# Which engine waits for the last stores: the closing wait of a ReLU row-sum kernel put on VectorE in place of SyncE

## Chip, cores and metric

One core of one Trainium2 chip. The metric is the device time of an execution in microseconds. Every run whose state is on record was in the fast state, with a granted clock of 1.00; of the first six runs of the kernel before, only the profiled one lists more than its time. Each of the other runs also lists its span, the time from the first to the last recorded instruction, to 0.1 us. The time is always longer than the span; "time outside the span" below is the one minus the other, so in a single timed run it is only good to 0.05 us.

## The reference

```python
# x: 32 x 512 x 1024 float32
relu_x = np.maximum(x, 0)
return np.sum(relu_x, axis=-1)      # 32 x 512
```

## The kernel before

67 MB come in, 64 KB go out. SyncE issues all loads and stores; ScalarE clamps, VectorE sums, and near the end each takes single rows with a fused clamp and sum. The end of the program is written by hand, without the usual closing barrier. The parts that the change and the argument touch:

```python
    def store(m, n, act, dve):
        nonlocal n_store
        dst, src = sums(m, n)
        nc.sync.wait_ge(sems.act, act)
        nc.sync.dma_start(out=dst, in_=src).wait_op(sems.dve, dve, "sem-ge").then_inc(
            sems.stored, 16
        )
        n_store += 1
    # ... cut: loads, clamps, sums ...
    store(0, ROWS, *freed[0])
    store(ROWS, NT - ROWS - 2, *sums_done)
    # ... cut: VectorE's last pieces of the last row but one ...
    store(NT - 2, 2, n_act, n_dve)
    return n_store

# the end of the program (line 45 and line 46):
    nc.sync.sem_clear(cleared)                    # loads, act and dve back to 0
    nc.sync.wait_ge(sems.stored, 16 * n_stores).then_inc(sems.stored, -16 * n_stores)
```

Three stores raise `stored` by 16 each. The last line waits for 48 and takes the 48 off again, so that the next execution finds the semaphore at 0.

Of the kernel before, what the change touches and what calls it, by code (L numbers as in the profile page):

```python
# [25 lines left out]
def kernel(tc: tile.TileContext, x: bass.AP, out: bass.AP):  # L26
    nc = tc.nc
    sems = Semaphores(tc)

    tc.close()  # L30
    tc.compile()
    nc.cur_bb = nc.bb_map[tc.start_bb_name]
    body = nc.cur_bb.bb.instructions
    ends = list(body)
    body.clear()
    n_stores = relu_sum(nc, sems, x, out)
    body.extend(ends)


    nc.cur_bb = nc.bb_map[tc.start_bb_name + "_end"]  # L40
    nc.cur_bb.bb.instructions.clear()
    nums = sorted(s.num for s in (*sems.loads, sems.act, sems.dve))
    cleared = range(nums[0], nums[-1] + 1)
    assert len(cleared) == len(nums)
    nc.sync.sem_clear(cleared)
    nc.sync.wait_ge(sems.stored, 16 * n_stores).then_inc(sems.stored, -16 * n_stores)
    issue_ahead_of_the_barrier(tc, EARLY)


# [183 lines left out]
def issue_ahead_of_the_barrier(tc: tile.TileContext, n_loads: int):  # L233


    SP = mybir.EngineType.SP
    blocks = tc.nc.main_func.blocks
    opening = blocks[0].instructions
    body = next(b for b in blocks if b.name == tc.start_bb_name).instructions
    loads = [i for i in body if i.engine == SP][:n_loads]  # L240
    for i in loads:
        assert isinstance(i, mybir.InstDMACopy)
        body.remove(i)
    at = next(n for n, i in enumerate(opening) if i.engine == SP)
    opening[at:at] = loads
# [30 lines left out]
```

## Time and profile before

| | before |
|---|---|
| time, median (lowest to highest), 3 runs | 161.35 us (161.24 to 161.53) |
| span of the profiled run | 159.63 us |
| time of that same run | 160.99 us, so 1.36 us outside the span |
| last input has landed | about 155.3 us |
| last sum ready, last store issued | 158.17, 158.19 us |
| wait of line 46 begins, ends | 159.615, 159.632 us |

How to read it: the input stream fills the span up to 155 us, and some work on the last rows follows. From 158.2 us on no engine computes; the core waits for one 1 KB store to be confirmed. The bar of a wait shows only its last few nanoseconds, after the semaphore has been satisfied; the waiting itself has no bar and must be read from the gap before it. Outside the span no instruction is recorded and no view of the profile shows anything.

### The profile page before, as it was taken

How to read it: one execution, taken by the hardware profiler on the slowest of the kernel's cores; microseconds unless marked ns; L12 is line 12 of the kernel's file. 1: busy time of each engine (PE TensorE's matmuls, PEld its weight loads, DVE VectorE, ACT ScalarE, POOL GpSimd, SP SyncE). 2: the span in 40 equal slices, each digit the busy share in tenths (PEclk: the TensorE clock that was granted, in tenths of full speed). 3: DMA queues.
4: the chain of work that ended last, by engine and by line, in shares of the span. 5: the costliest groups of instructions: out<-in, count | busy, mean ns of one | idle time of the engine just before them, and what ended most of it. 6: DMA issues, size and time to landing. Idle time of an engine off the chain costs nothing.

```text
span 159.6 us, 129 instructions
## 1 busy us (share of the span) xinstructions
DVE 117.5 (74%) x41; ACT 104.2 (65%) x50; POOL 0.2 (0%) x4
## 2 busy tenths in 40 slices
DVE  0000000009999499994999999999999999999986
ACT  3000059990799708996099941999339992499985
POOL 0000000000000000000000000000000000000000
DMA  7996996996996998979969969969969969798994
GB/s 263 525 525 263 525 526 263 525 525 263 526 493 296 525 411 378 525 328 460 526 279 509 525 263 526 525 263 525 525 263 525 509 279 525 337 452 386 412 405 127
DMA packets 2304, 67.18 MB, mean 421 GB/s; under 512 B 640, under 2 KB 896, under 8 KB 1024
## 3 DMA queue, kind: packets, MB, share of 16 engines
q1 hardware_dynamic: 2304, 67.18, 98.1%
HBM read 67.11 MB, written 0.07 MB: 421 GB/s over the span
## 4 chain that ended last, share of the span: by engine, by line
DMA 43%; DVE 34%; ACT 17%; another core or an unknown queue 3%; SPq 0%; issue 0%; DVEq 0%
DMA io<-in_x_dram 43%; DVE res L123 32%; ACT io L115 17%; DVE io L140 1%; SPq L97 0%; DVE piece L219 0%; DVE piece L140 0%; DVEq L218 0%
## 5 line engine op out<-in xcount | busy, mean ns | idle before, releaser
L123 DVE TENSOR_REDUCE res<-io 128x8 f32<-128x8192 f32 (+2 forms) x9 | 101.1, 11286 | 39.9 <-ACT io L115 39.9
L115 ACT ACTIVATE io<-io 128x8192 f32<-128x8192 f32 (+2 forms) x9 | 81.7, 9111 | 46.9 <-DMA io<-in_x_dram 46.9
L130 ACT ACTIVATE io<-io 128x1024 f32<-128x1024 f32 x20 | 20.9, 1045 | 5.9 <-DMA io<-in_x_dram 5.7
L140 DVE TENSOR_SCALAR_CACHE_REDUCE io<-io 128x1024 f32<-128x1024 f32 (+1 forms) x14 | 15.5, 1165 | 0.7 <-DMA io<-in_x_dram 0.6
L130 ACT ACTIVATION_READ_ACCUMULATOR io<-io 128x1 f32 x20 | 3.8, 188 | 0.0
L115 ACT ACT_TABLE_LOAD x1 | 1.3, 1283 | 0.8 <-PEq L260 0.8
L140 DVE DVE_READ_ACCUMULATOR io<-io 128x1 f32 x14 | 1.2, 82 | 0.0
L219 DVE TENSOR_SCALAR_CACHE_REDUCE piece<-piece 128x406 f32<-128x406 f32 x1 | 0.6, 576 | 0.1
L140 DVE TENSOR_SCALAR_CACHE_REDUCE piece<-piece 128x260 f32<-128x260 f32 x1 | 0.4, 424 | 0.0
L260 POOL MEMSET const-bfloat16-1.0<- 128x1 bf16 x1 | 0.1, 102 | 0.0
L260 POOL MEMSET const-uint8-127<- 128x1 uint8 x1 | 0.1, 102 | 0.0
L260 POOL MEMSET const-float32-0.0<- 128x1 f32 x1 | 0.1, 99 | 0.2 <-issue 0.2
L260 POOL MEMSET const-float32-1.0<- 128x1 f32 x1 | 0.1, 99 | 0.0
L140 DVE DVE_READ_ACCUMULATOR piece<-piece 128x1 f32 x1 | 0.1, 83 | 0.0
L219 DVE DVE_READ_ACCUMULATOR piece<-piece 128x1 f32 x1 | 0.1, 82 | 0.0
## 6 DMA issues: line engine op xcount, KB each, us to landing
io<-in_x_dram SPq DMA_DIRECT2D x1, 4096.0 KB, 21.6
io<-in_x_dram SPq DMA_DIRECT2D x1, 2048.0 KB, 26.1
io<-in_x_dram SPq DMA_DIRECT2D x1, 1204.0 KB, 28.6
io<-in_x_dram SPq DMA_DIRECT2D x1, 512.0 KB, 29.4
piece<-in_x_dram SPq DMA_DIRECT2D x1, 202.0 KB, 29.3
piece<-in_x_dram SPq DMA_DIRECT2D x1, 130.0 KB, 29.3
io<-in_x_dram SPq DMA_DIRECT2D x7, 26.9
out_dram<-res SPq DMA_DIRECT2D x1, 55.0 KB, 1.6
```

Of the source, the lines that this page charges most:

```text
L115: i = nc.scalar.activation(out=ap, in_=ap, func=RELU)
L123: nc.vector.tensor_reduce(out=res[:, m : m + n], in_=ap, axis=mybir.AxisListType.X, op=ADD).wait_op(sems.act, n_act, "sem-ge").then_inc(se ...
L130: i = nc.scalar.activation(out=ap, in_=ap, func=RELU, accum_out=res[:, m : m + 1])
L140: i = nc.vector.tensor_scalar(out=ap, in0=ap, scalar1=0.0, scalar2=None, op0=MAX, op1=ADD, accum_out=accum_out,)
L219: nc.vector.tensor_scalar(out=last[:, :], in0=last[:, :], scalar1=0.0, scalar2=None, op0=MAX, op1=ADD, accum_out=res[:, NT - 2 : NT - 1],) ...
L260: nc = _bacc.Bacc("TRN2", target_bir_lowering=False, num_devices=1)
```

## The change

The closing wait moves from SyncE's queue to VectorE's. VectorE has nothing left to do by then, and SyncE, which issued the stores, is freed about a microsecond sooner.

```diff
     nc.sync.sem_clear(cleared)
-    nc.sync.wait_ge(sems.stored, 16 * n_stores).then_inc(sems.stored, -16 * n_stores)
+    nc.vector.wait_ge(sems.stored, 16 * n_stores).then_inc(sems.stored, -16 * n_stores)
     issue_ahead_of_the_barrier(tc, EARLY)
```

## The prediction

> **What bounds the kernel now.** I read the head of the page first, then the chain that ended last, then the last stretch of the timeline, then the waits of SyncE's queue, then the single line that the change edits.
>
> ```profile
> span 159.6 us, 129 instructions
> DMA 43%; DVE 34%; ACT 17%; another core or an unknown queue 3%; SPq 0%; issue 0%; DVEq 0%
> DMA io<-in_x_dram 43%; DVE res L123 32%; ACT io L115 17%; DVE io L140 1%; SPq L97 0%; DVE piece L219 0%; DVE piece L140 0%; DVEq L218 0%
> ```
>
> These are the span and the chain, by engine and by line. The chain is the loads of x, ScalarE's clamp (L115) and VectorE's row sums (L123): 43 + 32 + 17 = 92% of the span. Over the span the DMA moves 67.18 MB at a mean of 421 GB/s, and its row of 40 slices stands at 9 almost everywhere, so the input stream sets the length up to about 155.4 us. The change touches none of that. It edits one instruction behind the last store, so only the last few microseconds are of interest. The timeline of them:
>
> ```profile
> 157.37 0.08 DVE L140 DVE_READ_ACCUMULATOR piece<-piece 128x1 f32 x1
> 157.58 0.58 DVE L219 TENSOR_SCALAR_CACHE_REDUCE piece<-piece 128x406 f32<-128x406 f32 x1
> 158.09 0.08 DVE L219 DVE_READ_ACCUMULATOR piece<-piece 128x1 f32 x1
> 158.19 0.33 SPq L108 DMA_DIRECT2D out_dram<-res  x1
> ```
>
> VectorE's last result is there at 158.09 + 0.08 = 158.17. SyncE issues the last store, of 1 KB, at 158.19. VectorE has nothing more to do, and ScalarE has finished before it. The waits of SyncE's queue in this stretch:
>
> ```profile
> SPq L107 <- ACT io L130: 28.2, 2, 27.3
> SPq L46 <- SPq L46: 1.0, 1, 1.0
> SPq L108 <- DVE piece L219: 0.3, 1, 0.3
> ```
>
> L46 is the line that changes. It waits 1.0 us, once. The view names the queue itself as the releaser, which cannot be literally true: what raises the semaphore is the landing of the last store, as the program says (three stores of 16 each, and the wait is for 48). The instruction itself:
>
> ```profile
> L46 SPq EVENT_SEMAPHORE  x1: 17/17/17, 159.6 to 159.6; - x1
> ```
>
> It takes 17 ns and begins when the wait is over: the trace puts its start at 159.615 and its end at 159.632, which is the end of the span. So the last 1.46 us of the span (158.17 to 159.63) are: 0.03 us to release the issue, about 1.42 us from the issue of the last store to the semaphore (the list of DMA issues has 1.4 for this store), 17 ns for the wait. SyncE's other instruction in that time, the range clear of L45, begins at 158.57 and takes 57 ns; it is over 0.99 us before the semaphore is full. It is hidden.
>
> **What the skill says.** The Trainium skill, page "DMA: Bandwidth & Descriptors", section "Anatomy of one DMA — SWDGE (gpsimd) path", puts most of a DMA's fixed cost of about 2 us into the receipt of the write at the target, which must come before the semaphore is raised. The trace agrees in kind: in this 1 KB store the packets run from about 0.83 us to 1.03 us after the issue began, and the semaphore is full 0.39 us later; the sum is 1.42 us and not 2.0. None of it depends on who waits.
>
> The page "Perfetto Trace Analysis", section "Sequencer-only Instruction (DRAIN, etc)", says that the profile shows such an instruction from the moment its semaphores are satisfied, so neither the wait nor the spreading of its own update is in the bar. The trace agrees: L46 is a bar of 17 ns behind a wait of 1.0 us. A wait on VectorE would be of the same kind.
>
> The page "Runtime: NRT & Kernel Launch", section "The ~15µs preamble/postamble breakdown", says that behind the kernel comes a barrier in which all engines meet (about 1.5 us), then a reset of semaphores, and that the serpentine over the five engines costs 44 ns a hop, some 355 ns in all. The trace shows no instruction behind L46, so it can neither confirm nor deny this. What it does show: the profiled run was timed at 160.99 us with a span of 159.63, so 1.36 us of the time lie outside the span, and what stands there is unknown to me.
>
> **The change, part by part.**
>
> Removed: one SyncE wait, 17 ns at the end of the span. Added: one VectorE wait with the same semaphore, threshold and decrement. VectorE's sequencer has done such a wait already:
>
> ```profile
> L218 DVEq EVENT_SEMAPHORE  x1: 21/21/21, 157.5 to 157.5; - x1
> ```
>
> 21 ns, against 17 on SyncE: +4 ns. The other cost is how fast each engine sees the semaphore. The opening barrier releases them in one go: SyncE's wait begins at 0.708, ScalarE's at 0.713, VectorE's at 0.719 from the start of the span, so VectorE is 11 ns later. A second comparison: the wait of L218 begins 38 ns after VectorE's read of 157.37 ended, and SyncE's store 28 ns after VectorE's last: 10 ns again. So the added end is 4 + 11 = +15 ns inside the span: 159.63 to about 159.65. VectorE is free from 158.17, its sequencer has only a branch left, and the semaphore comes at 159.6: it will be waiting in good time, with 1.4 us to spare. No reduction is delayed, because the wait stands behind the last one in VectorE's order.
>
> Moved: SyncE is now finished at about 158.57 + 0.06 = 158.63 and not at 159.63, 1.0 us sooner; VectorE is finished at 159.65 and not at 158.17. The last engine to finish does so at the same moment within 15 ns. The order on memory is unchanged: the range clear still comes behind the last store's own waits, and the stores' semaphore is still taken down only after all have landed. I see no race.
>
> Sum inside the span: +0.015 us, that is +0.01%. Outside the span: unknown in sign. If the engines meet afterwards in a chain, it matters how far along the chain the last engine stands, and whether SyncE has something of its own to do before it. By the skill's figure for the whole serpentine I estimate at most 0.35 us either way. A change like this in a tuned kernel is tried because someone hopes for exactly that, so I lean slightly to a gain, -0.06 us, a judgement and not a working. 161.35 + 0.015 - 0.06 is about 161.3 us.
>
> **Rivals.**
>
> First, SyncE's freedom is worth the whole 1.0 us: it would do work of its own behind the kernel while the store still flies. For it: 1.36 us outside the span are unexplained, and SyncE carries all DMA queues of this kernel. Against it: whatever ends the program must wait for VectorE too, and the store's landing is as late as before. It would give about 160.3 us, still within 1%. I give it under one in twenty.
>
> Second, VectorE is a worse place: the meeting point passes it early and must now go round again, or the first instructions behind the kernel are slower to come on VectorE than on SyncE. For it: SyncE was quickest to answer in the opening barrier, and the order of the others followed by 5, 6 and 2 ns. Against it: all those differences are tens of nanoseconds. It would give up to 161.35 + 0.35 = 161.7 us.
>
> Third, nothing changes outside the span, and the time is 161.35 + 0.015, 161.37 us, which three runs cannot tell from before. This is the likeliest of the three.
>
> None of them puts a load or a reduction on another schedule, because the edit lies behind all of them. That is also why no new bound can appear: VectorE is at 74% of the span and gets 21 ns more.
>
> **Range and chances.** The three runs before lie between 161.24 and 161.53, and the profiled run at 160.99; the spread of the same program is therefore 0.54 us, more than the effect that I expect. A median of three runs should move by less, some 0.2 us, and the unknown part outside the span adds up to 0.35 either way. I put the range at 160.85 to 161.7 us. The threshold of 2% is 3.2 us, more than twice the whole stretch from the last store's issue to the end; no way of this change leads there. Faster by over 2%: 0.005; within 2%: 0.99; slower by over 2%: 0.005.
>
> **What would show it.** In the profile after: a wait of about 21 ns on VectorE's queue as the last record, 1.4 us after the issue of the last store, and SyncE's last record the range clear; the span 159.6 to 159.7 unless the loads themselves ran differently; everything before 158 the same. The step outside the span is judged by the difference between the timed run and its span, 1.36 us now: if it is lower by several tenths, the first rival holds; if higher, the second. The prediction is wrong if the time leaves the range; then the cause must lie outside the span, or in a wait on VectorE that begins much later than 30 ns after the landing.

## The result and the profile after

| | before | after |
|---|---|---|
| time, median (lowest to highest) | 161.34 us (161.16 to 161.53), 6 runs | 161.38 us (161.30 to 161.59), 6 runs |
| ratio | | 1.0004, 95% interval 0.9992 to 1.0017 |
| span of the profiled run | 159.63 us | 159.81 us |
| time outside the span, that run | 1.36 us | 161.30 - 159.81 = 1.49 us |
| last store issued to wait begins | 1.420 us | 1.433 us |

A ratio here and below is the mean time of one kernel's runs over the mean of the other's of the same rounds, so it is not quite the ratio of the medians that stand beside it.

The head and the chain of the page of the kernel after, in shares of the span:

```profile
span 159.8 us, 129 instructions
DMA 43%; DVE 34%; ACT 17%; another core or an unknown queue 3%; SPq 0%; issue 0%; DVEq 0%
```

The same count of instructions and the same chain. The last microseconds of its timeline (start, length, engine, line, operation):

```profile
157.75 0.58 DVE L219 TENSOR_SCALAR_CACHE_REDUCE piece<-piece 128x406 f32<-128x406 f32 x1
158.25 0.08 DVE L219 DVE_READ_ACCUMULATOR piece<-piece 128x1 f32 x1
158.36 0.33 SPq L108 DMA_DIRECT2D out_dram<-res  x1
```

All three bars stand 0.16 us later than before (157.75 against 157.58) and are as long as they were. That shift has nothing to do with the edit. It is already there at the first load, whose semaphore is full at 21.71 us before and at 21.86 after. The chain in order of time, first of the kernel before and then of the kernel after:

```profile
0.79 40.24 DMA io<-in_x_dram
```

```profile
0.79 40.40 DMA io<-in_x_dram
```

The first load in the chain, which starts 159 us ahead of the edited instruction, took 40.40 us in place of 40.24. One profile against one profile thus shows a difference of 0.18 us in the span, of which 0.16 are the chance of the input stream. With an effect this small, measure from the last common event, here the issue of the last store, and not from the start.

The edited line of the kernel after:

```profile
L46 DVEq EVENT_SEMAPHORE  x1: 21/21/21, 159.8 to 159.8; - x1
```

It is on VectorE's queue and takes 21 ns, where it took 17 on SyncE. The trace puts its start at 159.792, its end at 159.813, the end of the span. The waits of SyncE's queue in the last five microseconds, after:

```profile
SPq L107 <- ACT io L130: 28.2, 2, 27.3
SPq L108 <- DVE piece L219: 0.3, 1, 0.3
```

The line "SPq L46 <- SPq L46: 1.0" that the prediction showed is gone. No line for it appears among VectorE's waits, though VectorE's queue stands idle from about 158.3 to 159.8. The landing did not become quicker; this view merely does not count the wait there.

What remained to explain was the other number, 1.49 us outside the span against 1.36, from one profiled run of each.

### The profile page after: what moved, and what is told of

It is laid out like the page before. It is cut to its first block, busy times and chain, and to the rows that moved or that the text cites. A ratio compares the mean times of both kernels' runs of the same rounds, so it can differ in the third digit from the quotient of the medians.

```text
span 159.8 us, 129 instructions
## 1 busy us (share of the span) xinstructions
DVE 117.5 (74%) x41; ACT 104.2 (65%) x50; POOL 0.2 (0%) x4
## 4 chain that ended last, share of the span: by engine, by line
DMA 43%; DVE 34%; ACT 17%; another core or an unknown queue 3%; SPq 0%; issue 0%; DVEq 0%
DMA io<-in_x_dram 43%; DVE res L123 32%; ACT io L115 17%; DVE io L140 1%; SPq L97 0%; DVE piece L219 0%; DVE piece L140 0%; DVEq L218 0%
```

## The experiments

All were run with repeated rounds beside the kernel before, on the same chip within a group. The groups ran on three chips. The kernel before had, outside its span, 1.378 us on average in the first group (11 runs), 1.377 in the second (9), 1.388 in the third (9), so this quantity is steady where the time itself varies by half a microsecond.

### First group: who waits

**before_again and after_again**: no edit; both kernels once more.

> The kernel before once more, for what its earlier runs did not list: the span of every run, so that the time outside the span can be had for each. In the one profiled run it was 160.99 - 159.63 = 1.36 us. If the engine that ends last matters outside the span (the rival), this stays near 1.36 while the changed kernel has about 1.5. If only the landing matters (my theory), both have the same mean within 0.05 us, and 1.36 was one run's chance. Time ratio to before 1.000.

> The changed kernel once more, on the same chip as before_again. My theory: VectorE's wait begins 1.42 to 1.45 us after the issue of the last store, time outside the span equal to that of before_again within 0.05 us, ratio 1.000. The rival that the place of the last engine matters: 1.49 us outside, as in its first six runs (1.48 to 1.53), and so +0.1 us on before_again.

**wait_on_act and wait_on_pe**: one edit each on the changed kernel.

```diff
-    nc.vector.wait_ge(sems.stored, 16 * n_stores).then_inc(sems.stored, -16 * n_stores)
+    nc.scalar.wait_ge(sems.stored, 16 * n_stores).then_inc(sems.stored, -16 * n_stores)
```

```diff
-    nc.vector.wait_ge(sems.stored, 16 * n_stores).then_inc(sems.stored, -16 * n_stores)
+    nc.tensor.wait_ge(sems.stored, 16 * n_stores).then_inc(sems.stored, -16 * n_stores)
```

> The same wait on ScalarE, which is idle at the end. My theory: last wait 1.42 to 1.45 us after the issue of the last store and the same time outside the span, ratio 1.000 within 0.0015. The rival that the place of the last engine in the meeting behind the kernel matters: a time outside the span that differs from SyncE's and from VectorE's by 0.05 us or more.

> The same wait on TensorE, which has done nothing in the kernel; in the opening barrier its wait took 51 ns where VectorE's took 21 and SyncE's 17. My theory: the span ends 30 to 40 ns later than with SyncE, the time outside is the same, ratio 1.000 within 0.0015. The rival that the place matters: time outside the span differs by 0.05 us or more.

| run | wait on | time, median (runs) | ratio to before (95%) | issue to start of wait | bar of wait | mean outside span |
|---|---|---|---|---|---|---|
| before_again | SyncE | 161.19 us (5) | 0.9997 (0.9985 to 1.0009) | 1.418 us | 17 ns | 1.364 us |
| after_again | VectorE | 161.41 us (5) | 1.0013 (1.0000 to 1.0026) | 1.435 us | 21 ns | 1.506 us |
| wait_on_act | ScalarE | 161.42 us (6) | 1.0017 (1.0004 to 1.0029) | 1.417 us | 17 ns | 1.547 us |
| wait_on_pe | TensorE | 161.64 us (5) | 1.0023 (1.0011 to 1.0035) | 1.419 us | 51 ns | 1.656 us |

The profiles of wait_on_act and wait_on_pe, line 46:

```profile
L46 ACTq EVENT_SEMAPHORE  x1: 17/17/17, 159.8 to 159.8; - x1
```

```profile
L46 PEldq EVENT_SEMAPHORE  x1: 51/51/51, 160.0 to 160.0; - x1
```

The semaphore is seen 1.417 to 1.435 us after the issue by all four: the landing does not care who waits for it. Inside the span, engines differ by tens of nanoseconds. Outside, they differ by up to 0.29 us. My theory had bet on equality within 0.05 us and falls: the five runs of after_again lie between 1.49 and 1.53 us, the five of before_again between 1.32 and 1.39. The rival of the last engine's place stands so far.

### Second group: the wait itself, or who ends last

**wait_on_pool**: the same one-line edit, with `nc.gpsimd`.

> The same wait on GpSimd, the last engine not yet tried. Theory now (place of the last engine): time outside the span is neither SyncE's 1.37 us nor equal for all; it fits a line of engines in which SyncE is nearest to the end and TensorE farthest, so between 1.37 and 1.66 us, and I guess 1.42 to 1.50, between SyncE and VectorE. The rival that the extra 0.13 us comes from SyncE having been freed early, not from where the last engine stands: 1.50 to 1.55, as for VectorE and ScalarE. A value below 1.37 would make it the best engine for the wait.

**late_sync_after**: the wait stays on VectorE, but SyncE is kept busy until after it.

```diff
     nc.sync.sem_clear(cleared)
+    for _ in range(30):
+        nc.sync.sem_clear(cleared)
     nc.vector.wait_ge(sems.stored, 16 * n_stores).then_inc(sems.stored, -16 * n_stores)
```

> The changed kernel with 30 more range clears on SyncE behind its own, so that SyncE ends last again, after VectorE's wait. If a clear comes every 65 ns, SyncE ends about 2.4 us after the issue of the last store, some 0.9 us after VectorE. Place of the last engine: time outside the span falls back to 1.37 us (SyncE's), although the wait is still on VectorE. The rival that a wait standing on VectorE costs 0.13 us by itself, say because VectorE's own work behind the kernel is slower: 1.50 us, or in between.

**slack_sync_after**: the same with `range(10)`, so that SyncE still ends before VectorE.

> The changed kernel with 10 more range clears on SyncE: some 0.65 us in the microsecond that the change freed, so SyncE still ends before VectorE. Place of the last engine: span unchanged, 1.50 us outside, time as after_again (ratio to before 1.001). The rival that SyncE uses its freedom for work of its own behind the kernel: the time rises by up to 0.65 us, outside 1.6 us or more.

**late_vector**: VectorE is kept busy behind its wait.

```diff
     nc.vector.wait_ge(sems.stored, 16 * n_stores).then_inc(sems.stored, -16 * n_stores)
+    for _ in range(30):
+        nc.vector.sem_clear(cleared)
```

> The changed kernel with 30 range clears on VectorE behind its wait, so that the end of VectorE is known to be the end of all, by some 2 us. Place of the last engine: the span grows by the whole length of the clears (about 2 us) and 1.50 us stay outside, as without them. The rival that part of the time outside is hidden behind something of fixed length: outside falls below 1.4 us and the time grows by less than the clears.

| run | ends last | time, median (runs) | ratio to before (95%) | span, profiled run | mean outside span |
|---|---|---|---|---|---|
| wait_on_pool | GpSimd | 161.76 us (5) | 1.0035 (1.0022 to 1.0048) | 159.97 us | 1.932 us |
| late_sync_after | SyncE | 162.60 us (5) | 1.0082 (1.0069 to 1.0096) | 161.25 us | 1.388 us |
| slack_sync_after | VectorE | 161.26 us (5) | 1.0007 (0.9994 to 1.0019) | 159.84 us | 1.498 us |
| late_vector | VectorE | 166.40 us (4) | 1.0321 (1.0307 to 1.0336) | 164.90 us | 1.462 us |

The decisive run is late_sync_after. Its two lines (47: the added clears; 48: the wait, moved down by the edit):

```profile
L47 SPq EVENT_SEMAPHORE_RANGE_CLEAR  x30: 48/48/52, 158.9 to 161.2; - x30
L48 DVEq EVENT_SEMAPHORE  x1: 21/21/21, 159.9 to 159.9; - x1
```

VectorE's wait is over at 159.90 and SyncE ends at 161.25, 1.35 us later. The time outside falls from VectorE's 1.50 to 1.388 us, SyncE's value. So it is not the wait standing on VectorE that costs the 0.13 us; it costs them only if VectorE is the last to end. (The added length itself missed my expectation of 0.9 us, because a clear comes every 79 ns and not every 65.)

In slack_sync_after the added clears end about 0.23 us before VectorE does:

```profile
L47 SPq EVENT_SEMAPHORE_RANGE_CLEAR  x10: 48/48/52, 158.9 to 159.6; - x10
L48 DVEq EVENT_SEMAPHORE  x1: 21/21/21, 159.8 to 159.8; - x1
```

Its outside is 1.498 us, as for the kernel after without them. The median of 161.26 looks like no loss against the 161.26 of the kernel before on that chip, but one of its runs stands at 161.74 and the interval holds both answers; the outside is the better gauge. SyncE's freed microsecond can thus be filled or left empty with no effect: SyncE uses it for nothing that shortens the program.

wait_on_pool refutes my guess: I had put GpSimd between SyncE and VectorE, at 1.42 to 1.50 us, and it is by far the farthest, at 1.93 us, although its own bar is as short as SyncE's:

```profile
L46 POOLq EVENT_SEMAPHORE  x1: 17/17/17, 160.0 to 160.0; - x1
```

late_vector lengthened the span by 5.1 us and not by 2, and the outside stayed at 1.46 us. The rival had asked for a time that grows by less than the clears: the time grew by 166.41 - 161.23 = 5.18 us between the means, the span by 164.95 - 159.86 = 5.09. So at most 0.04 us of what lies outside went under the clears; where they went stands below, under "Behind the last instruction".

The 5.1 us came as a surprise. SyncE stepped through thirty such instructions at 79 ns each, VectorE at 174 on average (159 as a rule, and one gap of 578). That gave another explanation: perhaps the outside is nothing but each engine's own steps behind the kernel, at its own pace.

### Third group: pace or place, and the landing

**late_act, late_pool, late_pe**: late_vector's edit with `nc.scalar`, `nc.gpsimd` and `nc.tensor` in both lines.

> The wait on ScalarE with 30 range clears behind it, to have the pace at which ScalarE's sequencer steps through such instructions, which was 79 ns each on SyncE and 174 ns on VectorE. The rival that the extra time outside the span (0.13 us VectorE, 0.17 ScalarE, 0.28 TensorE, 0.55 GpSimd, over SyncE) is the slower pace of that engine's own instructions behind the kernel: in proportion, 79 + 0.17/0.13 x 95, about 200 ns on ScalarE. Place of the last engine in a line: the pace has nothing to do with it and may be SyncE's, near 79 ns, as its wait of 17 ns was. Outside the span about 1.50 to 1.55 us by both.

> The wait on GpSimd with 30 range clears behind it. Pace of the engine: 79 + 0.55/0.13 x 95, about 480 ns a clear, and a span some 14 us longer. Place in a line: a pace that does not fit that order, for example near 79 ns as its wait of 17 ns was. Outside the span 1.85 to 1.95 us by both; a fall to 1.4 would mean that GpSimd's 0.55 us are spent beside the clears, as something GpSimd does only when it is first left idle.

> The wait on TensorE with 30 range clears behind it. Pace of the engine: 79 + 0.28/0.13 x 95, about 280 ns a clear. Place in a line: any other pace, above all one slower than GpSimd's or faster than VectorE's. Outside the span 1.60 to 1.66 us by both.

**no_last_store**: the changed kernel without its last store, so wrong; VectorE then waits for 32.

```diff
-    store(NT - 2, 2, n_act, n_dve)
+    nc.sync.wait_ge(sems.act, n_act)
+    nc.sync.wait_ge(sems.dve, n_dve)
     return n_store
```

> The changed kernel without its last store, wrong on purpose: the last two sums of each partition are never written. SyncE still waits for the sums and VectorE for the two stores that are left; the second of these lands at about 158.4 us. The landing of the last store sets the end, whoever waits: the span shrinks by about 1.4 us to 158.4 to 158.5, the time falls to about 159.9 us, ratio 0.991 to 0.993. The rival that the 1.4 us are something else at the end, which the store only covers: the time falls by less than 0.5 us.

The thirty clears (line 48) in the profiles of late_vector, late_act, late_pool and late_pe, one fence each:

```profile
L48 DVEq EVENT_SEMAPHORE_RANGE_CLEAR  x30: 130/130/130, 159.7 to 164.8; - x30
```

```profile
L48 ACTq EVENT_SEMAPHORE_RANGE_CLEAR  x30: 97/98/98, 159.8 to 163.6; - x30
```

```profile
L48 POOLq EVENT_SEMAPHORE_RANGE_CLEAR  x30: 111/111/117, 160.1 to 164.1; - x30
```

```profile
L48 PEldq EVENT_SEMAPHORE_RANGE_CLEAR  x30: 149/151/151, 159.9 to 166.1; - x30
```

The first and last start, divided by 29, give the mean pace; the trace gives the usual one, without the odd long gap.

| engine | usual pace of a clear | mean pace | outside over SyncE's, wait only | outside behind 30 clears |
|---|---|---|---|---|
| SyncE | 79 ns | 79 ns | 0 | 1.388 us (late_sync_after) |
| ScalarE | 122 ns | 133 ns | +0.17 us | 1.538 us |
| GpSimd | 138 ns | 138 ns | +0.55 us | 1.893 us |
| VectorE | 159 ns | 174 ns | +0.13 us | 1.462 us |
| TensorE | 212 ns | 214 ns | +0.28 us | 1.586 us |

(The fourth column is each mean less 1.38 us, the mean outside of the kernel before in the first two groups.) Pace alone falls. It asked for 480 ns on GpSimd and for ScalarE slower than VectorE; GpSimd has 138 and ScalarE is quicker than VectorE. Yet GpSimd pays four times what VectorE pays. My other expectation, that ScalarE and GpSimd would go at SyncE's pace because their wait bars are as short as SyncE's, was wrong as well. The times were 165.33, 165.98 and 167.93 us, ratios 1.0261, 1.0298 and 1.0423, all from the clears; the outside of each engine came again within 0.01 to 0.07 us of its value without them. TensorE's 1.586 us is just below the 1.60 to 1.66 that I had expected.

no_last_store took 160.08 us, ratio 0.9935 (0.9922 to 0.9947), 1.05 us less than the kernel before on that chip (161.13 us in the mean), where I had expected about 1.4 us less and a ratio of 0.991 to 0.993. The rival with less than 0.5 us is out: the landing of the last store is most of the last 1.4 us. What takes its place is readable. The lines 46 and 45 in its profile:

```profile
L46 DVEq EVENT_SEMAPHORE  x1: 21/21/21, 158.5 to 158.5; - x1
```

```profile
L45 SPq EVENT_SEMAPHORE_RANGE_CLEAR  x1: 69/69/69, 158.6 to 158.6; - x1
```

VectorE's wait for the second store, issued at 156.79, begins at 158.53 in the trace, 1.74 us after that issue and not 1.6 as I had reckoned; SyncE, which goes through a wait at 158.37, a branch at 158.43 and its range clear, ends last at 158.66. And the time outside is 1.364 us, SyncE's value again, in a kernel whose store wait is VectorE's. It fits the rule that the last to end decides but is no clean second witness: VectorE ended only 0.11 us earlier, less than its surplus of 0.13 us, so that 158.55 + 1.50 and 158.66 + 1.38 come to the same.

No version with a correct result beat the kernel before. Of the five places for the wait, SyncE's is the best, and that is where it was.

### Behind the last instruction: what the kept traces hold

The trace that each run left (`trace.npz`) also lists the times at which every semaphore changed, and that list goes on behind the last instruction; no view of the profile prints it. Semaphore 2, which the kernel does not use, changes there in two rounds of short steps. The last step of all comes 1.47 to 2.04 us behind the end of the span. In all 14 profiled runs that is 0.109 to 0.119 us more than the measured time outside. Why it is more is not known, since the trace does not mark where the timed execution begins and ends; but the difference is constant to 10 ns, while the time outside itself varies by 0.58 us. So the surplus lies behind the last record.

| ends last (run) | outside, that run | end of span to first step | steps in first round | first to last of them | from there to last step of all |
|---|---|---|---|---|---|
| SyncE (before) | 1.358 us | 0.132 us | 5 | 0.162 us | 1.183 us |
| VectorE (after) | 1.487 us | 0.175 us | 6 | 0.243 us | 1.181 us |
| GpSimd (wait_on_pool) | 1.927 us | 0.567 us | 7 | 0.285 us | 1.185 us |
| ScalarE (wait_on_act) | 1.538 us | 0.144 us | 8 | 0.322 us | 1.188 us |
| TensorE (wait_on_pe) | 1.667 us | 0.232 us | 9 | 0.355 us | 1.190 us |

The last column is the same for all, to 0.01 us (of the other nine runs only late_pe, with 1.145 us, differs by more). The engines differ in two terms: how long the last engine takes to its first step, and how much of the round is still to come. The trace does not name the engine that takes a step; I infer it from the counts. Nine steps follow when TensorE ends last, and one fewer for each next engine. In the kernel before, the four that are missing behind the span stand inside it, at 1.003, 157.912, 157.950 and 158.313 us: the second 0.11 us after ScalarE's last record, the fourth 0.15 us after VectorE's. So the engines meet in a line, TensorE, ScalarE, GpSimd, VectorE, SyncE, and four more steps end the round.

VectorE's surplus over SyncE is then a first step that comes 0.043 us later and 0.081 us more of the round, together 0.124 of the 0.13 us. GpSimd's is 0.435 + 0.123 = 0.558 us: its place in the line is indeed next to VectorE's, and my guess for wait_on_pool failed on the 0.567 us that it takes to its step. In late_sync_after VectorE's step falls inside the span, at 160.077 us, and behind the span follow only 0.113 and 0.164 us, close to SyncE's values. Behind thirty clears the first step comes 31 to 40 ns sooner on the four other engines than behind the wait alone (0.140 in place of 0.175 us on VectorE), which is most of the way from 1.50 us to late_vector's 1.46.

## Why the prediction was right or wrong, point by point

- **The range and the class were right.** 161.38 us lies in 160.85 to 161.7, and the change is within 2%. The range is 0.85 us wide, more than five times the effect found, so holding it says little about the mechanism.
- **The path was read rightly.** The landing of the last 1 KB store, not the waiting engine, fills the last 1.4 us: 1.417 to 1.435 us from issue to wait in the seven profiled runs without added instructions that end with this wait on one engine or another, and a kernel without that store is a microsecond shorter.
- **+0.015 us inside the span was right.** Measured from the issue to the end of the wait: 1.433 + 0.021 = 1.454 us after, 1.420 + 0.017 = 1.437 before, so +17 ns. A single run is not finer than that, though: on VectorE the wait began at 1.433, 1.435 and 1.433 us, in late_sync_after at 1.427 and in late_vector at 1.420. Counted in the trace from the last change of the stores' semaphore, the wait begins after 16 and 17 ns on SyncE (two runs) and after 27 to 29 ns on VectorE (six runs). So both terms hold, the bar's 4 ns and the 11 ns of later notice.
- **The step outside the span was the one that failed.** The prediction left its sign open and leaned to a gain of 0.06 us, with the reason that someone who tries such a thing hopes for it. That is no reason from a profile. Measured: 1.50 us in after (means of 1.502 and 1.506) against 1.38 in before (1.378, 1.377, 1.388), +0.13 us. The thought beside it was sound: the engines do meet in a chain, and the place of the last one in it counts. The bound of 0.35 us held for VectorE; for GpSimd, at +0.55, it would not have held, because it left out the time that an engine takes to its first step.
- **Of the rivals, the third was called the likeliest and was wrong; the second was right in direction and in kind.** Both grounds of the second have a share: more of the round is still to come behind VectorE (0.081 us), and its first step comes later (0.043 us). That the third's 161.37 us lies 0.01 us from the measured 161.38 is luck of the input stream, as the point on the time shows. The first, that SyncE's freedom is worth up to 1.0 us, is refuted by the time itself, which did not fall, and by slack_sync_after.
- **Three readings of the prediction do not hold.** It found that the trace agrees in kind with most of a DMA's fixed cost lying in the receipt of the write. In this store 0.83 us pass from the issue to the first packet, and only 0.38 from the end of the last packet to the full semaphore (1.02 and 1.40 us after the issue). It took the trace to be silent on what follows L46; the instruction records are, the semaphore times are not. And the hidden range clear ends 0.985 us before the wait of L46 begins, not over 0.99.
- **Why the time hardly shows it.** The cost is 0.13 + 0.015, about 0.15 us or 0.09%. In the first comparison the means were 161.418 and 161.347 us, +0.07. In the first group they were 161.426 and 161.215, +0.21: 0.13 outside and 0.08 in the span, of which the wait explains under 0.02. The rest is the input stream, as in the two profiles. The time alone could not have decided the sign in six runs; the split at the end of the span did.
- **What stays open.** What the engines do between their last record and their first step, above all GpSimd in its 0.53 to 0.57 us, and what fills the 1.18 us after the first round beside the second round. It is shown, by late_sync_after, that VectorE's surplus goes when SyncE ends well after it; that the pace of its sequencer does not by itself set the order; and, by the semaphore times, that the surplus lies behind the last record. Which engine takes which step of the line is inferred, not recorded.

## What to carry to other kernels

When the edit sits at the end of a program, split the time into span and rest, and measure the span from the last common event: here that separated 0.015 us, 0.13 us and the noise of the loads, which the time mixes. Where no bar is left, look whether the trace still holds semaphore times. The engine that ends last has a price that no bar shows; the same wait cost 0 on SyncE, +0.13 us on VectorE and +0.55 us on GpSimd in this program, so leave it on SyncE, in a program like this one, unless a run says otherwise. Freeing an engine early is worth nothing if no work is there for it.

## What the Trainium skill lacked or had wrong

- "Runtime: NRT & Kernel Launch", section "The ~15µs preamble/postamble breakdown", gives one figure for the closing barrier and 44 ns a hop, but nothing on which engine had best arrive last. Here it mattered: 1.38 us outside the span with SyncE last, 1.50 VectorE, 1.55 ScalarE, 1.66 TensorE, 1.93 GpSimd. The semaphore times agree with its sum and its mean: nine steps take 0.355 to 0.358 us, in the first round when TensorE ends last and in the second of every run. But single hops take 23 to 100 ns. The 355 ns of its whole serpentine, which I took as a bound, are less than GpSimd's surplus of 0.55 us, and it has nothing on the time to an engine's first step, 0.13 us on SyncE and 0.57 on GpSimd.
- No page that I found has the pace at which each engine steps through range clears: 79 ns on SyncE, 122 ScalarE, 138 GpSimd, 159 VectorE, 212 TensorE. "Trainium Kernel Development and Optimization", section "NeuronCore Architecture", lists SyncE, ScalarE and GpSimd all at 1.2 GHz; their paces of 79, 122 and 138 ns differ all the same.
- "DMA: Bandwidth & Descriptors", section "Anatomy of one DMA — SWDGE (gpsimd) path", puts the fixed cost of a DMA at about 2 us for the path through GpSimd. That section has no such sum for a DMA that SyncE issues. Here the semaphore of a 1 KB store by SyncE was full 1.40 us after the issue; a 55 KB one took 1.6, and 1.7 in no_last_store.
